# GpSimd issues the key pages of a paged attention cache, the sync engine the values

## The chip, the cores and the metric

The kernel runs on one core of one Trainium2 chip. The metric is the device time of one execution in microseconds. Five engines work at once, each on its own in-order stream of instructions: TensorE (PE; its weight loads are shown as PEld), VectorE (DVE), ScalarE (ACT), GpSimd (POOL) and SyncE (SP, which here only issues transfers). SP, ACT and POOL can issue DMAs. They are carried out by 16 DMA engines, which share the work of all queues.

## The reference, cut to what matters

One inference step of a two-layer decoder. Layer 0 is stick-breaking attention, layer 1 a diagonal state-space layer, and a gated MLP with a short convolution follows each. A prompt group (512 tokens) and a sample group (8 sequences of 8 new tokens, each with 2048 cached tokens) run through the same weights. The change touches the part in which the sample group reads its cache of 128 pages, 16 for each sequence. A page is 128 keys x 16 heads x 64 floats, 512 KB, and there is as much of values:

```
page_table = permutation(n_pool)[:8 * 16].reshape(8, 16)
k_all = cache_k[0][page_table]          # (8, 2048, 16, 64), values alike
z = (q . k) / 8 + bias                  # per head
log_keep = log_sigmoid(-z)              # causal
between = cumsum(log_keep, reverse) - log_keep
o = exp(log_sigmoid(z) + between) @ v
```

The scan over keys runs from the last key to the first, so the keys of a page must stand in their order along the columns of the scores.

## The kernel before, in words

In `attention_layer`, `sample_cache` (a generator) walks over the 128 pages in pairs. For page i, `load_k(i)` takes a buffer `kp` (128 partitions x 4 x 256 floats, one of KBUF = 4) and fills it by four DMAs, one for each quarter j. A quarter holds four of the 16 heads, 1 KB of each key, and goes to the 32 partitions 32j to 32j+31, four keys to a partition. By KSPLIT (line 45), SP issues the quarters 0, 1 and 2, and GpSimd quarter 3. Before that, each of the two reads the page's number from the table into a register (`page_id`). `load_v(i)` lets GpSimd issue one DMA of 512 KB into `vp` (one of VBUF = 4), 4 KB for each of 128 partitions.

`turn(i)` lets VectorE transpose `kp` in blocks of 32 x 32 into `kt` (two buffers, line 425), and then calls `load_k(i + 4)`, which has to wait for this transpose since it fills the same buffer. TensorE forms the scores z of a page in 16 matmuls (line 447). ScalarE takes two sigmoids of them (lines 455, 456), VectorE scans and multiplies (459, 460), TensorE transposes the weights back (469), ScalarE copies them (471), and TensorE multiplies them with the values into `po` (478). At line 457 GpSimd sets the one column `left[:, 256:]` to 1.0, from which the scan starts. At the end of a pair's round, `load_v` is called for the pair that reuses its `vp` buffers, and these wait for the products at line 478.

This stream runs beside the prompt's work: the generator `prompt_pair` and others are companions that the large matmuls step on by `tick`, so that on TensorE the small products of the sample lie between the large products of the prompt, in an order fixed at build time. TensorE works in that order: when the keys of a page are late, everything behind them on TensorE is late too. The projection weights come in units of 512 KB through SP (`load_unit`, line 169, three `raw` buffers), split into a high and a low half by ScalarE (140) and VectorE (141). A planner's simulated times set the order of each engine's instructions, so SP's stream mixes key quarters, weights and output rows. After the first pages, `raws["last"]` is the last DMA that SP issued for the keys, and later weight loads on SP are put behind it.

The stream starts at the end of the kernel's first 20 us. Its last pages are dealt with in the first MLP, `ffn(0, ...)`, which calls `between`, and from there `finish_sample`.

Of the kernel before, what the change touches and what calls it, by code (L numbers as in the profile page):

```python
# [17 lines left out]
P = 128  # L18
# [23 lines left out]
RAWX, KAFTER, XPRI, XN = 3, 1, 1, 2  # L42
QENG = 1
GUNITS = 0, 2, 4, 6
KSPLIT, VQ = (('SP', (0, 1, 2)), ('G', (3,))), 'G'
WEAVE, NPERIOD, IPERIOD = 2700, 6000, 1200
BIG = 4
ASTEPS, AEND = 44, 20
# [6 lines left out]
SB = {"gemm": 3, "tr": 2, "vy": 3}  # L55
SHARE = {"up": "vy"}
EARLY = 2
RL = 2
XA, XB = 0, 2
RAWU = 3, 4  # L60
QGROUPS = [[0, 1], [2, 3]]
# [31 lines left out]
def hybrid_kernel(  # L93
# [9 lines left out]
    V, S, G, T, SP = nc.vector, nc.scalar, nc.gpsimd, nc.tensor, nc.sync  # L103
# [46 lines left out]
    raws = {"pool": glob, "bufs": NRAW, "n": -1, "last": None, "chain": True, "views": {}}  # L150
# [50 lines left out]
    def norm_rows(xs, rows, gain, room=rows_tile, inplace=False):  # L201

        hs = [room()] * len(xs) if inplace else [room() for x in xs]
        ss = const.tile([P, len(xs)], F32, name="ss", tag="ss", bufs=3)
        for i, x in enumerate(xs):
            S.activation(hs[i][:rows], x, AF.Square, accum_out=ss[:rows, i:i + 1])
        r = rsqrt(const, ss, len(xs), rows, 1.0 / D, "nr", 3)
        if inplace:
            hs = xs
        for i, x in enumerate(xs):  # L210
            V.scalar_tensor_tensor(hs[i][:rows], x, r[:rows, i:i + 1], gain[:rows], ALU.mult, ALU.mult)
        return hs
# [86 lines left out]
    def attention_layer(sp, sps):  # L299
# [53 lines left out]
        def queries(b, eng=G):  # L353
            t = Qb[b % 2]
            for j in range(4):
                (eng.copy if eng == S else eng.tensor_copy)(t[32 * j:32 * j + 32, :, DS * j:DS * j + DS], Qc[32 * j:32 * j + 32, :, b * DS:(b + 1) * DS])
            return t
# [20 lines left out]
        def columns(ptag, perm):  # L378

            ps = sps.tile([P, 8, NS], F32, name="psc", tag=ptag, bufs=2)  # L380
            for c in range(8):
                T.transpose(ps[:, c, :], perm[:NS, c].rearrange("p j r -> p (j r)"), ident[:NS, :NS])
            return ps
# [3 lines left out]
        last_dma = {}  # L387

        def page_id(eng, idx):

            with tc.issue_after(last_dma[eng].ins) if eng in last_dma else nullcontext():
                return eng.value_load(idx, min_val=0, max_val=cache_k.shape[1] - 1)

        def sample_cache():

            pages = [(b, m, e) for b in range(DB) for m in range(NPG // 2 - 1, -1, -1) for e in (1, 0)]
            kps, kts, vps = {}, {}, {}
            Q = prev = po = before = None

            def number(i):  # L400
                b, m, e = pages[i]
                return pt[0:1, b * NPG + 2 * m + e:b * NPG + 2 * m + e + 1]

            def load_k(i):
                if i < len(pages):
                    kps[i] = sp.tile([P, 4, 256], F32, name="kp", tag="kp", bufs=KBUF)

                    for eng, js in KSPLIT:
                        eng = {'SP': SP, 'G': G, 'S': S}[eng]
                        r = page_id(eng, number(i))  # L410
                        page = cache_k[0, bass.ds(r, 1)].rearrange("o (kk kb) (j h) d -> j (o kk) kb (h d)", j=4, kb=4)
                        for j in js:
                            last_dma[eng] = eng.dma_start(kps[i][32 * j:32 * j + 32], page[j])  # L413

            def load_v(i):
                if i < len(pages):
                    vps[i] = sp.tile([P, D], F32, name="vp", tag="vp", bufs=VBUF)
                    eng = {'SP': SP, 'G': G, 'S': S}[VQ]
                    r = page_id(eng, number(i))
                    last_dma[eng] = eng.dma_start(vps[i], cache_v[0, bass.ds(r, 1)].rearrange("o k h d -> (o k) (h d)"))  # L420

            def turn(i):
                if i < len(pages):
                    kts[i] = sp.tile([P, 4, 8, 32], F32, name="kt", tag="kt")
                    V.transpose(kts[i].rearrange("p a c k -> p (a c k)"), kps.pop(i).rearrange("p a c -> p (a c)"))  # L425
                    load_k(i + KBUF)

            for i in range(KBUF):
                load_k(i)
            yield  # L430
            for i in range(2):
                load_v(i)
                turn(i)
            for i in range(0, len(pages) + 2, 2):
                if i < len(pages):
                    b, m, _ = pages[i]
                    start = m == NPG // 2 - 1
                    if start:
                        Q = queries(b, G if i or not QENG else S)

                    z = sps.tile([P, 512], F32, name="z", tag="sz", bufs=2)
                    for e in (1, 0):
                        x = i + 1 - e
                        kt = kts.pop(x)
                        for half in range(2):
                            for h in range(4):
                                T.matmul(z[32 * h:32 * h + 32, e * P:(e + 1) * P].rearrange("p (k a) -> p a k", a=4),  # L447
                                         Q[:, 2 * h + half, :], kt[:, :, 2 * h + half, :], start=half == 0, stop=half == 1)
                        turn(x + 2)
                        if e:  # L450
                            yield
                    sg = sp.tile([P, 256], F32, name="sg", tag="sg")

                    left = sp.tile([P, 257], F32, name="left", tag="left")
                    S.activation(left[:, :256], z[:, :256], AF.Sigmoid, bias=nbias_r, scale=-0.125)
                    S.activation(sg, z[:, :256], AF.Sigmoid, bias=bias_r, scale=0.125)
                    G.memset(left[:, 256:], 1.0)
                    back = left[:, ::-1]
                    V.tensor_tensor_scan(back, back, back, 1.0 if start else prev[:, 0:1], ALU.mult, ALU.min)
                    V.tensor_tensor(sg, sg, left[:, 1:], ALU.mult)  # L460
                    prev = left
                    now = i, b, m, z, sg
                    yield
                else:
                    now = None
                if before:
                    i0, b0, m0, z0, sg0 = before
                    for e in range(2):
                        T.transpose(z0[:, (2 + e) * P:(3 + e) * P], sg0[:, e * P:(e + 1) * P], ident)
                    wT = sp.tile([P, 2, P], F32, name="wT", tag="wT")  # L470
                    S.copy(wT.rearrange("p e f -> p (e f)"), z0[:, 256:])  # L471
                    yield
                    if m0 == NPG // 2 - 1:
                        po = sps.tile([P, 256], F32, name="po", tag="so")
                    for e in (1, 0):
                        v = vps.pop(i0 + 1 - e)
                        for h in range(4):
                            T.matmul(po[32 * h:32 * h + 32].rearrange("p (j d) -> p j d", j=4),  # L478
                                     wT[:, e, 32 * h:32 * h + 32],
                                     v.rearrange("p (j h d) -> p h j d", j=4, h=4)[:, h],  # L480
                                     start=m0 == NPG // 2 - 1 and e == 1, stop=m0 == 0 and e == 0)
                    if m0 == 0:
                        o = sp.tile([P, 256], F32, name="o", tag="wT")
                        S.copy(o, po)
                        S.dma_start(o_scr[:, b0], o)
                    yield
                for x in range(i + 2, i + 4):
                    load_v(x)
                before = now
# [206 lines left out]
        with pool_(name="start", bufs=2) as wp, pool_(name="start_ps", bufs=5, space=PSUM) as psp:  # L696
# [9 lines left out]
            with tc.high_priority():  # L706
# [8 lines left out]
                h, = norm_rows([xres[NT][:NS]], NS, gain)  # L715
# [31 lines left out]
            sample_query(1)  # L747
            raws["chain"] = False
            stream = sample_cache()
            with tc.issue_after(raws["last"].ins) if KAFTER else nullcontext():  # L750
                next(stream)
            raws["last"] = (None, raws["last"], last_dma[SP])[RL]
            ps = columns("sz", perm)
            with tc.high_priority():
                V.tensor_copy(Qc, ps)
# [949 lines left out]
    samp = sctx.enter_context(pool_(name="samp", bufs=2, side="right"))  # L1705
    samp_ps = sctx.enter_context(pool_(name="samp_ps", bufs=1, space=PSUM, side="right"))
    finish_sample, start = attention_layer(samp, samp_ps)

    def between():
# [36 lines left out]
```

## Time and profile before

| | |
|---|---|
| median of 3 runs | 1868.32 us (1867.57 to 1873.78) |
| the profiled execution's own time | 1855.74 us |
| its span, first to last instruction | 1854.0 us |
| mean granted TensorE clock | 0.962 of full speed |
| TensorE, VectorE, ScalarE, GpSimd busy | 92%, 62%, 39%, 20% of the span |
| moved by DMA | 297.42 MB, 160 GB/s over the span |

The page has one row for each engine with its busy time, and rows that cut the span into 40 equal slices, each digit a busy share in tenths; PEclk is the clock that TensorE was granted. The waits view tells for each engine at which line it sat idle and what ended that. The windows view gives busy time, the granted clock, the busy share of the 16 DMA engines and the bytes that they moved, for any stretch. The share can come out a little over 1.

### The profile page before, as it was taken

How to read it: one execution, taken by the hardware profiler on the slowest of the kernel's cores; microseconds unless marked ns; L12 is line 12 of the kernel's file. 1: busy time of each engine (PE TensorE's matmuls, PEld its weight loads, DVE VectorE, ACT ScalarE, POOL GpSimd, SP SyncE). 2: the span in 40 equal slices, each digit the busy share in tenths (PEclk: the TensorE clock that was granted, in tenths of full speed). 3: DMA queues.
4: the chain of work that ended last, by engine and by line, in shares of the span. 5: the costliest groups of instructions: out<-in, count | busy, mean ns of one | idle time of the engine just before them, and what ended most of it. 6: DMA issues, size and time to landing. Idle time of an engine off the chain costs nothing. (4 is left out here: it accounts for less than half of the span.)

```text
span 1854.0 us, 35632 instructions
## 1 busy us (share of the span) xinstructions
PE 1706.5 (92%) x12754; PEld 1419.9 (77%) x12754; DVE 1152.0 (62%) x2016; ACT 726.9 (39%) x1392; POOL 369.6 (20%) x676
## 2 busy tenths in 40 slices
PE   5988889989898998997999899899999999999999
PEld 3766566666545785896888889789878989989897
DVE  7445676676776666798668786765446544444443
ACT  5323434444443363432334534445433423323231
POOL 3132222222221110066123232001010100000000
PEclk8989999989988997998999999999999999999999
DMA  8799999999999682624375736455322322232221
GB/s 253 197 245 261 261 253 249 259 261 255 265 257 234 159 220 93 170 72 130 106 144 155 186 119 163 124 162 160 119 86 69 92 81 86 76 92 80 81 80 64
DMA packets 303301, 297.42 MB, mean 160 GB/s; under 512 B 58520, under 2 KB 250993, under 8 KB 303124
## 3 DMA queue, kind: packets, MB, share of 16 engines
q1 hardware_dynamic: 277074, 209.89, 43.1%
q0 software_dynamic: 24896, 84.20, 16.7%
q8 instruction: 101, 1.65, 0.4%
q10 hardware_dynamic: 1154, 1.05, 0.2%
q14 instruction: 76, 0.62, 0.1%
HBM read 268.93 MB, written 26.13 MB: 159 GB/s over the span
## 5 line engine op out<-in xcount | busy, mean ns | idle before, releaser
L862 PE MATMUL up<-hT,whi 128*128 128x256 f32 (+2 forms) x1344 | 407.3, 303 | 10.9 <-DVE gf L982 5.4
L141 DVE TENSOR_TENSOR wlo<-raw,whi 128x1024 fp32r<-128x1024 f32 x203 | 253.2, 1250 | 253.3 <-ACT whi L140 249.4
L863 PE MATMUL up<-hT,whi 128*128 128x256 f32 (+2 forms) x1344 | 403.4, 300 | 0.0
L864 PE MATMUL up<-hT,wlo 128*128 128x256 f32 (+2 forms) x1344 | 403.0, 300 | 0.0
L140 ACT CAST whi<-raw 128x1024 fp32r<-128x1024 f32 x206 | 215.3, 1048 | 351.4 <-PE up L863 151.0
L862 PEld LDWEIGHTS up<-hT,whi 128*128 128x128 f32 x1344 | 256.9, 191 | 20.1 <-DVE gf L982 6.9
L863 PEld LDWEIGHTS up<-hT,whi 128*128 128x128 f32 x1344 | 257.0, 191 | 3.1 <-issue 0.6
L864 PEld LDWEIGHTS up<-hT,wlo 128*128 128x128 f32 x1344 | 256.9, 191 | 1.5
L425 DVE STREAM_TRANSPOSE kt<-kp 128x1024 f32<-128x1024 f32 x128 | 157.9, 1238 | 145.4 <-DMA kp<-in_cache_k_dram 109.6
L447 PE MATMUL z<-kt,Qb 128*32 128x128 f32 x2048 | 100.4, 291 | 50.2 <-DVE kt L425 43.4
L268 PE MATMUL dn<-whi,g 128*128 128x512 f32 x352 | 137.3, 401 | 7.8 <-DVE xres L1059 5.0
L269 PE MATMUL dn<-wlo,g 128*128 128x512 f32 x352 | 140.8, 400 | 0.3 <-DVE wlo L141 0.3
L270 PE MATMUL dn<-whi,g 128*128 128x512 f32 x352 | 139.1, 398 | 0.0
L968 POOL COPY cst<-apad 128x2 f32<-128x2 f32 x44 | 36.7, 835 | 497.8 <-ACT apad L956 497.8
L447 PEld LDWEIGHTS z<-kt,Qb 128*32 128x32 f32 x2048 | 62.6, 114 | 78.5 <-DVE kt L425 40.0
L413 POOL DMA_DIRECT2D kp<-in_cache_k_dram x128 | 73.0, 571 | 238.7 <-DVE kt L425 99.7
L420 POOL DMA_DIRECT2D vp<-in_cache_v_dram x128 | 72.1, 563 | 187.6 <-PE po L478 118.2
L268 PE MATMUL psg<-whi,hT 128*128 128x256 f32 (+1 forms) x320 | 105.8, 332 | 0.3 <-DVE slo L606 0.3
L269 PE MATMUL psg<-wlo,hT 128*128 128x256 f32 (+1 forms) x320 | 103.9, 325 | 0.0
L270 PE MATMUL psg<-whi,hT 128*128 128x256 f32 (+1 forms) x320 | 102.4, 323 | 0.0
L478 PE MATMUL po<-vp,wT 128*32 128x256 f32 x1024 | 90.9, 414 | 0.8 <-ACT wT L471 0.4
L268 PEld LDWEIGHTS dn<-whi,g 128*128 128x128 f32 x352 | 66.2, 189 | 25.5 <-DVE xres L1059 5.9
(482 smaller groups left out, 3345.2 us busy)
## 6 DMA issues: line engine op xcount, KB each, us to landing
vp<-in_cache_v_dram POOLq DMA_DIRECT2D x128, 512.0 KB, 8.8
kp<-in_cache_k_dram SPq DMA_DIRECT2D x384, 128.0 KB
raw<-in_ffn_w_up_dram SPq DMA_DIRECT2D x96, 512.0 KB
raw<-in_ffn_w_down_dram SPq DMA_DIRECT2D x48, 512.0 KB
kp<-in_cache_k_dram POOLq DMA_DIRECT2D x128, 128.0 KB, 7.4
raw<-in_attn_w_qkv_dram SPq DMA_DIRECT2D x64, 128.0 KB
raw<-in_attn_w_o_dram SPq DMA_DIRECT2D x16, 512.0 KB
raw<-in_ssm_w_glu_dram SPq DMA_DIRECT2D x32, 256.0 KB
```

The lines of the kernel that those rows point to most:

```text
L140: S.copy(hi, src)
L141: eng.tensor_tensor(lo, src, hi.bitcast(F32), ALU.subtract)
L268: T.matmul(ps, x[0], whi, start=st, stop=False)
L269: T.matmul(ps, x[0], wlo, start=False, stop=False)
L270: T.matmul(ps, x[1], whi, start=False, stop=sp_)
L413: last_dma[eng] = eng.dma_start(kps[i][32 * j:32 * j + 32], page[j])
L425: V.transpose(kts[i].rearrange("p a c k -> p (a c k)"), kps.pop(i).rearrange("p a c -> p (a c)"))
L447: T.matmul(z[32 * h:32 * h + 32, e * P:(e + 1) * P].rearrange("p (k a) -> p a k", a=4), Q[:, 2 * h + half, :], kt[:, :, 2 * h + half, :], ...
L478: T.matmul(po[32 * h:32 * h + 32].rearrange("p (j d) -> p j d", j=4), wT[:, e, 32 * h:32 * h + 32], v.rearrange("p (j h d) -> p h j d", j= ...
L862: T.matmul(ps[:, :t1 - t0], w[0][:, k, :], hi, start=k == 0, stop=False)
L863: T.matmul(ps[:, :t1 - t0], w[0][:, k, :], lo, start=False, stop=False)
L864: last_mm["PE"] = T.matmul(ps[:, :t1 - t0], w[1][:, k, :], hi, start=False, stop=k == KC - 1)
```

## The change

GpSimd issues all four quarters of a key page, in the order 0, 2, 1, 3, and reads the page number once. The page in memory is described with other dimensions: key = 8n + a, with a, of size 8, outermost, and n, of size 16, inside it. As before, the elements fill the buffer in order, so that partition 4a + b of a quarter (b = 0 to 3) holds the keys 8n + a for n = 4b to 4b + 3. The matmul writes its columns so that the scores stand in the order of the keys again. SP issues the value pages. VectorE, not GpSimd, sets the column of `left`. `raws["last"]` becomes the last DMA of GpSimd.

```diff
-KSPLIT, VQ = (('SP', (0, 1, 2)), ('G', (3,))), 'G'
-RL = 2
...
-                    for eng, js in KSPLIT:
-                        eng = {'SP': SP, 'G': G, 'S': S}[eng]
-                        r = page_id(eng, number(i))
-                        page = cache_k[0, bass.ds(r, 1)].rearrange("o (kk kb) (j h) d -> j (o kk) kb (h d)", j=4, kb=4)
-                        for j in js:
-                            last_dma[eng] = eng.dma_start(kps[i][32 * j:32 * j + 32], page[j])
+
+                    r = page_id(G, number(i))
+                    page = cache_k[0, bass.ds(r, 1)].rearrange("o (n a) (j h) d -> j a (o n) (h d)", j=4, a=8)
+                    for j in (0, 2, 1, 3):
+                        last_dma[G] = G.dma_start(kps[i][32 * j:32 * j + 32], page[j])
...
-                    eng = {'SP': SP, 'G': G, 'S': S}[VQ]
-                    r = page_id(eng, number(i))
-                    last_dma[eng] = eng.dma_start(vps[i], cache_v[0, bass.ds(r, 1)].rearrange("o k h d -> (o k) (h d)"))
+                    r = page_id(SP, number(i))
+                    last_dma[SP] = SP.dma_start(vps[i], cache_v[0, bass.ds(r, 1)].rearrange("o k h d -> (o k) (h d)"))
...
-                                T.matmul(z[32 * h:32 * h + 32, e * P:(e + 1) * P].rearrange("p (k a) -> p a k", a=4),
-                                         Q[:, 2 * h + half, :], kt[:, :, 2 * h + half, :], start=half == 0, stop=half == 1)
+                                T.matmul(z[32 * h:32 * h + 32, e * P:(e + 1) * P].rearrange("p (b k a) -> p k a b", b=4, k=4),
+                                         Q[:, 2 * h + half, :], kt[:, :, 2 * h + half, :].rearrange("p k (a b) -> p k a b", b=4), start=half == 0, stop=half == 1)
...
-                    G.memset(left[:, 256:], 1.0)
+                    V.memset(left[:, 256:], 1.0)
...
-            raws["last"] = (None, raws["last"], last_dma[SP])[RL]
+            raws["last"] = last_dma[G]
```

## Rows read from the trace of the kernel before

**Rows 1.** The page: busy time by engine, and the DMA engines' share in 40 slices.

```profile
PE 1706.5 (92%) x12754; PEld 1419.9 (77%) x12754; DVE 1152.0 (62%) x2016; ACT 726.9 (39%) x1392; POOL 369.6 (20%) x676
...
DMA  8799999999999682624375736455322322232221
```

**Rows 2.** Windows: stretch, length, busy us (instructions) by engine, granted clock, DMA share, GB/s.

```profile
60.00:700.00 640.00, 570.51 (x5441) 401.79 (x5434) 415.49 (x657) 262.63 (x591) 156.03 (x344) 0.93 0.98 245
100.00:600.00 500.00, 438.27 (x4364) 297.43 (x4363) 327.35 (x500) 202.23 (x486) 131.56 (x288) 0.92 1.04 255
420.00:450.00 30.00, 30.00 (x287) 20.38 (x288) 23.32 (x38) 13.54 (x31) 9.57 (x21) 1.00 1.08 263
500.00:540.00 40.00, 33.58 (x294) 17.92 (x295) 27.18 (x38) 15.72 (x39) 11.56 (x27) 0.70 1.04 253
672.00:674.50 2.50, 2.50 (x23) 2.50 (x22) 2.50 (x3) 1.09 (x3) 0.36 (x2) 1.00 1.04 394
26.00:34.00 8.00, 5.55 (x16) 3.64 (x16) 6.23 (x9) 4.97 (x9) 4.58 (x5) 0.79 0.84 207
```

**Rows 3.** TensorE's waits from 60 to 700: total us, times, longest.

```profile
PE z L447 <- DVE kt L425: 43.4, 24, 5.1
```

**Rows 4.** What the transpose at line 425 waited for, 60 to 700: us, times.

```profile
  DMA kp<-in_cache_k_dram: 107.8, 48
```

**Rows 5.** DMA queues and issues, 60 to 700 (q0 GpSimd's, q1 SP's).

```profile
q1 hardware_dynamic: 89406, 72.35, 49.7%
q0 software_dynamic: 24000, 82.07, 47.2%
...
vp<-in_cache_v_dram POOLq DMA_DIRECT2D x126, 512.0 KB, 8.8
kp<-in_cache_k_dram SPq DMA_DIRECT2D x366, 128.0 KB
kp<-in_cache_k_dram POOLq DMA_DIRECT2D x122, 128.0 KB, 7.4
```

**Rows 6.** Queue q0 and what it issued, 672 to 674.5.

```profile
q0 software_dynamic: 206, 0.78, 81.5%
...
vp<-in_cache_v_dram POOLq DMA_DIRECT2D x1, 512.0 KB, 5.1
```

**Rows 7.** Lines 413 and 420 on GpSimd: durations in ns, min/median/max.

```profile
L413 POOL DMA_DIRECT2D kp<-in_cache_k_dram x118: 552/570/588, 62.1 to 639.3; - x118
...
L420 POOL DMA_DIRECT2D vp<-in_cache_v_dram x126: 537/563/574, 64.7 to 683.5; - x126
```

**Rows 8.** GpSimd's timeline: two issues back to back; a second value page.

```profile
24.86 1.10 POOL L413 DMA_DIRECT2D kp<-in_cache_k_dram  x2
...
104.57 0.56 POOL L420 DMA_DIRECT2D vp<-in_cache_v_dram  x1 [0.70 <-PE z L447]
```

**Rows 9.** GpSimd's waits, 60 to 700.

```profile
POOL vp L420 <- PE po L478: 118.2, 40, 32.7
...
POOL left L457 <- DVE left L459: 32.5, 18, 6.2
```

**Rows 10.** SP's timeline: a weight unit, and the MLP's first weights.

```profile
181.85 2.07 SPq L169 DMA_DIRECT2D raw<-in_attn_w_qkv_dram  x4
...
599.77 30.79 SPq L169 DMA_DIRECT2D raw<-in_ffn_w_up_dram  x5
```

**Rows 11.** GpSimd's timeline: the longest wait of a value page.

```profile
624.21 0.56 POOL L420 DMA_DIRECT2D vp<-in_cache_v_dram  x1 [32.66 <-PE po L478]
```

**Rows 12.** Lines by form, 60 to 700: busy us, mean ns, idle before.

```profile
L447 PE MATMUL z<-kt,Qb 128*32 128x128 f32 x2024 | 99.7, 291 | 50.2 <-DVE kt L425 43.4 <-DVE hn_ss L125 4.1 <-DVE rs_y L135 2.3
...
L469 PE MATMUL z<-ident,sg 128*128 128x128 f32 x128 | 29.5, 309 | 4.4 <-DVE sg L460 4.2
```

**Rows 13.** Line 457 on GpSimd, 60 to 700: durations in ns.

```profile
L457 POOL MEMSET left<- x62: 98/99/118, 70.3 to 678.9; 128x1 f32 x62
```

## The prediction, made blind

> **What bounds the kernel now.** I read the page first [rows 1]. TensorE is busy 92% of the span, but the row of slices shows something it doesn't have elsewhere: from slice 1 to slice 12 the DMA engines are full, and then never again. That is the stretch in which the sample reads its cache. So the windows come next [rows 2]: from 60 to 700 us TensorE is busy 570.5 of 640 us, idle 69.5, at a granted clock of 0.93; from 100 to 600 the DMA share is 1.04 at only 255 GB/s. Full engines need not mean full bandwidth, so I looked for stretches with other traffic. From 672 to 674.5, when the last key page has landed, the same share moves 394 GB/s, most of it a value page [rows 2, 6]. From 26 to 34, when the first key pages come in, 0.84 moves 207. Sixteen engines times share over rate gives the engine time of a megabyte: 16 x 1.04 / 255 = 65 us in the stage, 16 x 0.84 / 207 = 65 for the first key pages, 16 x 1.04 / 394 = 42 without keys. So it is the key quarters that make the transfers slow. The stage moves 72.35 + 82.07 MB and a little more [rows 5], 156.5 MB in all (245 GB/s x 640 us); at 65 us that is 156.5 x 65 / 16 = 636 us of all engines, which is the stage's length. The stage is as long as its transfers take.
>
> How this reaches TensorE is in the waits: the transpose of a page waited 107.8 us for keys, in 48 of 126 pages [rows 4], and TensorE 43.4 us for the transpose [rows 3]; with two waits in which another VectorE instruction came last, line 447 lost 50.2 of the 69.5 us [rows 12]. The clock is the second loss. Where no page is late TensorE is busy all the time at 1.00 (420 to 450), and in the worst part, 500 to 540, with 6.4 us idle, it is granted 0.70 [rows 2]. [...]
>
> **The change part by part.**
>
> *Keys.* Before, each of the 488 quarters in the stage is described with 32 groups of keys outermost on both sides, now with 8 on the side of the cache. If that makes 8 shares of it, consecutive quarters go to partitions 0 to 31, 64 to 95, 32 to 63, 96 to 127, and can run side by side, each on its own engines. No row shows a quarter dealt in this way. Its engine time per megabyte lies between 42 us (no keys, [rows 2]) and 65 (as now). What is needed is little: at the pace of a TensorE that never waits for keys, 640 - 50 = 590 us, the 156.5 MB may take 16 x 590 / 156.5 = 60 us a megabyte. I take a value under that, since GpSimd's own queue, whose traffic is four parts values and one part keys, already moves a megabyte in 0.472 x 16 x 640 / 82.07 = 59 us beside SP's 0.497 x 16 x 640 / 72.35 = 70 us [rows 5]. So keys no longer set the pace.
>
> [...]
>
> *What the lost wait is worth.* Of the 50 us at line 447 I count 37: three quarters, as VectorE, busy 415 of 640 us and in order, will be late for some pages itself. Of the 40 us of clock I count 18, somewhat under half, since low stretches follow idle ones and not all idling goes. Together 55; bounds 0 and 50 + 40 = 90.
>
> *GpSimd's queue.* It issues 4 x 128 quarters where it issued 128 quarters and 128 value pages: 256 more at 0.57 us [rows 7], 146 us, spread over 640 us in which it is busy 156. Two quarters one behind the other took 1.10 us, and a new page number costs 0.70 us [rows 8], so a page needs 4 x 0.57 + 0.70 = 3.0 us, against a page each 640 / 126 = 5.1 us, or 4.6 at the new pace. The last quarter goes out 1.7 us after the first. With four buffers a page is asked for three pages ahead, some 14 us, of which issue, landing (7.4 us now, [rows 5]) and transpose take 12. I take 0, and price the rest in the third rival. At the start twelve more quarters stand among GpSimd's weight splits: between 0 and 12 x 0.57 = 6.8 us, I take 0, as TensorE still has projections to do before its first keys.
>
> [...]
>
> *SP's queue.* It loses 384 issues and gets 128, and moving the values takes GpSimd's 118.2 us of waits for line 478 [rows 9] to SP. Behind a waiting value page now stand weight units, output rows, and the next value page; TensorE waits for the weights. A wait is 3 us on average (118.2 / 40), a unit is issued in about 2 us [rows 10], and the list of TensorE's waits in the stage names no weight tile; I take 0. The long wait, 32.7 us at 624 [rows 11], lies where the attention ends and five units of the MLP's weights go out between 600 and 631 [rows 10]. If they came behind it, up to 30 us would go back; the planner knows that wait and orders by it, so I take 0 and keep the 30 for the range. The value pages themselves need 5.1 to 8.8 us [rows 5, 6] and are asked for as soon as line 478 frees a buffer, two pairs ahead of their use.
>
> *The small edits.* 64 settings of a column move to VectorE: 0.10 us each on GpSimd [rows 13], 6 us of VectorE time if it is no faster, none where it waits anyway; with it go GpSimd's 32.5 us of waits at line 457 [rows 9], which would hold up keys. I take 0. The scores' columns are now written 32 elements apart, not 4: line 447, at a step of 4, takes 291 ns, line 469, at a step of 1, 309 [rows 12], so the step shows no price; 0. `raws["last"]` on GpSimd's queue orders nothing on SP; weights may go out ahead of the first pages: 0.
>
> **The sum.** The profiled execution took 1855.7 us, with 1.7 us around its span of 1854.0. Less 55 that is 1801. The median of the runs shown stands 12.6 us above that execution, so I say 1813.
>
> **The rivals.**
>
> *TensorE keeps much of its idling.* Keys come in time, but VectorE and ScalarE then end last at each step of the stream, and the clock stays low: gain 6 to 20 us, 1848 to 1862. For it: VectorE's 65%. Against it: the 30 us from 420 to 450 at 100% of TensorE and full clock with the same work [rows 2].
>
> *Nothing moves.* The engines are the bound by their number, or the reads of 1 KB from each key are what is slow and not their way in: 65 us a megabyte remain, 1868. For it: queue q1's rows are mostly such reads. Also here if the transfer isn't cut as I think.
>
> *GpSimd becomes the bound, or one half of the engines does.* The slower case is a quarter that costs GpSimd more than (5.1 - 0.7) / 4 = 1.1 us instead of 0.57; from there on pages come late however fast they land. At 1.3 us a page takes 5.9 and the stage 126 x 0.8 = 100 us more: 1970. Against it: 588 ns at most. The same side is reached if all quarters fall to the same eight engines: these would carry the keys, 64 MB, and half of the remaining 92.5, 110 MB, in 110 x 42 / 8 = 578 us at best, still no loss, but slower from 46 us a megabyte on; at 55 it is 756, and the time 1868 + 116 = 1984. No view shows which engines serve a DMA. I give GpSimd 0.07 and the half 0.05.
>
> **How the numbers follow.** The forecast, a gain of 20 to 100 us, gets 0.70, idling kept 0.08, nothing moves 0.10, the slower cases 0.12. What a measurement can tell from no change is 0.3%, 5.6 us. Faster takes 0.70, 0.08 and a little of the third: 0.80. Same 0.09, slower 0.11. The forecast's own range is 1778 (both bounds, 90 us) to 1848; below, 1768 would take the clock wholly back with what other idling there is. Upward I go to 1866, which takes in the kept idling and the 30 us of late weights; the slower cases, and most of "nothing moves", stay out.
>
> **What would show it.** Right: from 100 to 600 us on the old axis, a DMA share well under 1 at 270 GB/s or more; the transposes' wait for keys under 30 us; TensorE's wait at line 447 under 15; the granted clock from 60 to 640 at 0.96 or more; the end of the stage some 55 us earlier, and all behind it moved, not changed. Wrong: a share of 1 at 250 GB/s (nothing moves); GpSimd's issues longer than 1 us, or GpSimd with no idle time (it is the bound); SP waiting for line 478 with TensorE waiting for weights behind it.

## The result, and the profile after

The changed kernel takes 1798.74 us (median, 1791.93 to 1801.45), the kernel before beside it 1867.94: a ratio of 0.9643, 95% interval 0.9609 to 0.9676, so 69 us faster. 1813 was forecast. The profiled execution took 1791.93 us, its span 1790.2 against 1854.0. Lines have moved: 413 is now 410, 416 issues the values (420 before), 421 is the transpose (425), 443 the key product (447), 474 the value product (478), 453 the column of `left` (457), 455 the scan (459).

The page, busy time by engine and the DMA slices, answers to [rows 1]:

```profile
PE 1669.1 (93%) x12754; PEld 1401.0 (78%) x12754; DVE 1154.4 (64%) x2080; ACT 727.8 (41%) x1394; POOL 549.2 (31%) x868
...
DMA  8599888877899946233757454554222222232221
```

TensorE has the same 12754 matmuls and is busy 37.4 us less: they ran at full clock more often (mean granted clock 0.972, before 0.962). The other 26.4 of the 63.8 us of span were idle time (147.5 before, 121.1 now). The DMA engines now have spare time from the fifth slice to the eleventh.

Windows of the changed kernel, columns as in [rows 2]:

```profile
60.00:640.00 580.00, 537.87 (x5494) 386.47 (x5492) 420.07 (x710) 267.73 (x598) 327.86 (x528) 0.97 0.87 270
60.00:700.00 640.00, 580.37 (x5840) 415.56 (x5839) 461.19 (x829) 288.17 (x638) 327.86 (x528) 0.95 0.82 255
100.00:600.00 500.00, 474.59 (x4822) 341.48 (x4820) 380.63 (x656) 246.69 (x551) 284.05 (x459) 0.99 0.88 274
580.00:700.00 120.00, 78.16 (x805) 49.26 (x804) 73.99 (x170) 33.08 (x70) 34.18 (x53) 0.73 0.67 209
```

From 100 to 600 a megabyte now takes 16 x 0.88 / 274 = 51 us of engine time, not 65 [rows 2]. TensorE is busy 475 of 500 us there (438 before) at 0.99 of its clock (0.92). The last row is a loss that the kernel before doesn't have: TensorE is idle 42 us of 120, at 0.73 of its clock. This is called the tail below; the same stretch before, at the same columns:

```profile
580.00:700.00 120.00, 114.55 (x877) 91.49 (x874) 79.85 (x151) 55.01 (x94) 16.52 (x42) 0.99 0.76 200
```

VectorE's and TensorE's waits, 60 to 700 (us, times, longest), two queries of one view, answer to [rows 3, 4]:

```profile
DVE kt L421 <- DMA kp<-in_cache_k_dram: 6.5, 5, 3.6
...
PE po L474 <- ACT wT L467: 12.7, 15, 5.3
PE z L443 <- DVE kt L421: 9.1, 4, 3.5
```

The transposes wait 6.5 us for keys (107.8), TensorE 9.1 for the transpose (43.4); its wait for the attention weights that ScalarE copies, 12.7, is now longer than that. GpSimd's issues and the queues, answering to [rows 5, 7]:

```profile
L410 POOL DMA_DIRECT2D kp<-in_cache_k_dram x488: 647/647/663, 72.4 to 630.2; - x163
```

```profile
q1 hardware_dynamic: 63975, 96.83, 48.7%
q0 software_dynamic: 39040, 64.24, 32.5%
...
vp<-in_cache_v_dram SPq DMA_DIRECT2D x125, 512.0 KB, 6.0
kp<-in_cache_k_dram POOLq DMA_DIRECT2D x488, 128.0 KB, 5.2
```

Keys land in 5.2 us (7.4), values in 6.0 (8.8), while more bytes move in the same time (274 GB/s from 100 to 600, before 255).

Where TensorE's order went: the costliest group of the output projection, before from 600 to 640, and after from 440 to 480:

```profile
L270 PE MATMUL psg<-whi,o_lo 128*128 128x512 f32 x42 | 16.6, 395 | 0.0
```

```profile
L267 PE MATMUL psg<-wlo,o_hi 128*128 128x512 f32 x42 | 17.1, 408 | 0.0
```

The prompt's attention is done some 150 us earlier, while the last key product only moved from 682.9 to 638.0. In TensorE's instruction list 57.5 of 64 pairs of pages stood ahead of the output projection; now 39.5 do. This order is planned at build time, and it moves with the queue that issues what (43.5 in e6 below, 54 in e7); the planner had drawn the prompt's work ahead.

### The profile page after: what moved, and what is told of

Its sections match the earlier page's. It is cut to its first block, busy times and chain, and to the rows that moved or that the text cites. A ratio compares the mean times of both kernels' runs of the same rounds, so it can differ in the third digit from the quotient of the medians.

```text
span 1790.2 us, 34994 instructions
## 1 busy us (share of the span) xinstructions
PE 1669.1 (93%) x12754; PEld 1401.0 (78%) x12754; DVE 1154.4 (64%) x2080; ACT 727.8 (41%) x1394; POOL 549.2 (31%) x868
## 5 line engine op out<-in xcount | busy, mean ns | idle before, releaser
L410 POOL DMA_DIRECT2D kp<-in_cache_k_dram x512 | 331.6, 648 | 229.2 <-DVE kt L421 131.0
L266 PE MATMUL psg<-whi,hT 128*128 128x256 f32 (+1 forms) x320 | 100.6, 316 | 0.5 <-DVE hT L139 0.5
L267 PE MATMUL psg<-wlo,hT 128*128 128x256 f32 (+1 forms) x320 | 99.4, 311 | 0.0
L268 PE MATMUL psg<-whi,hT 128*128 128x256 f32 (+1 forms) x320 | 98.4, 309 | 0.0
L443 PE MATMUL z<-kt,Qb 128*32 128x128 f32 x2048 | 85.7, 291 | 9.1 <-DVE kt L421 9.1
L474 PE MATMUL po<-vp,wT 128*32 128x256 f32 x1024 | 77.6, 416 | 14.0 <-ACT wT L467 12.7
L443 PEld LDWEIGHTS z<-kt,Qb 128*32 128x32 f32 x2048 | 57.0, 116 | 32.9 <-issue 10.6
L267 PEld LDWEIGHTS dn<-wlo,g 128*128 128x128 f32 x352 | 66.7, 190 | 15.9 <-DVE wlo L139 0.7
```

Source lines behind the costliest of these rows:

```text
L266: T.matmul(ps, x[0], whi, start=st, stop=False)
L267: T.matmul(ps, x[0], wlo, start=False, stop=False)
L268: T.matmul(ps, x[1], whi, start=False, stop=sp_)
L410: last_dma[G] = G.dma_start(kps[i][32 * j:32 * j + 32], page[j])
```

## The experiments

All twelve have an interval from runs beside the kernel before, whose medians lie between 1865.3 and 1868.9 us in all sets. "A megabyte" is engine time, 16 x share / rate from 100 to 600. The traces of e3, e7 and e9 are of executions 15, 17 and 11 us above the medians in the table. The edits are given in short form, and "shares", as in the name of e1, are the parts into which I took one DMA to be divided among the engines: an assumption, since no view shows them or which engines serve a DMA.

| run | ratio, 95% interval | median us | a megabyte, us |
|---|---|---|---|
| changed kernel | 0.9643, 0.9609 to 0.9676 | 1798.74 | 51 |
| e1, 16 shares | 0.9833, 0.9796 to 0.9870 | 1836.88 | 61 |
| e2, neighbours | 0.9810, 0.9771 to 0.9850 | 1833.84 | 61 |
| e3, order 0, 1, 2, 3 | 0.9824, 0.9789 to 0.9860 | 1833.77 | 61 |
| e4, 8 groups, old queues | 1.0158, 1.0120 to 1.0196 | 1897.42 | 54 |
| e5, 16 groups, dealt | 0.9829, 0.9789 to 0.9869 | 1837.02 | 62 |
| e6, values moved only | 1.0138, 1.0097 to 1.0179 | 1888.30 | 62 |
| e7, SP quarter 3 | 1.0165, 1.0143 to 1.0188 | 1894.74 | 65 |
| e8, SP quarter 1 | 0.9940, 0.9918 to 0.9962 | 1855.74 | 60 |
| e9, order held | 0.9749, 0.9715 to 0.9784 | 1825.04 | 51 |
| e10, held, faster stream | 0.9877, 0.9847 to 0.9907 | 1847.30 | 50 |
| e11, held, 16 shares | 0.9885, 0.9845 to 0.9925 | 1847.01 | 62 |
| e12, memset on GpSimd | 0.9806, 0.9770 to 0.9841 | 1831.76 | 51 |

**e1, e2, e3, e5: what made the keys fast.** TensorE's order is that of the changed kernel in all four. e5 has 16 groups outermost, not 8 (key = 16n + a).

```diff
 e1 -j a (o n) (h d)", j=4, a=8      +"o (kk kb) (j h) d -> j (o kk) kb (h d)", j=4, kb=4
 e2 -"o (n a) (j h) d                +"o (a n) (j h) d
 e3 -for j in (0, 2, 1, 3):          +for j in (0, 1, 2, 3):
 e5 -j=4, a=8)                       +j=4, a=16)
```

> The changed kernel, but the key quarters are described with 32 groups of keys outermost again (4 neighbouring keys to a partition), and the matmul as before. All issues, their queues, their order 0, 2, 1, 3 and TensorE's order of instructions stay those of the changed kernel. Theory A (what made the transfers fast is that a quarter is dealt to 8 engines, each with its own way into its partitions, and two quarters run side by side): the gain from the rate goes, the engine time of a megabyte from 100 to 600 us rises from 51 us to 58 or more, the transposes wait for keys 60 us or more (6.5 in the changed kernel), time 1825 to 1880. Theory B (what made them fast is GpSimd's queue, which gathers the 1 KB reads into larger packets where SP's sends them one by one): the shares don't matter, 1799 +- 6.

> The changed kernel with 8 outermost, but each of the eight groups takes 16 neighbouring keys (key = 16a + n, not 8n + a); the matmul writes as before the change. Theory A: the way into the partitions is the same, 1799 +- 8. Rival C (the dealing of neighbouring keys to different engines is part of the gain, because the reads of a page then spread better): slower by 1% or more, 1817 and up, with a higher engine time per megabyte.

> The changed kernel with the quarters in the order 0, 1, 2, 3, nothing else. Theory A, with the engines taken eight at a time in turn: quarters 0 and 1 then go by two sets of engines into the same half of the ways in, so the rate falls to that of before, 58 us a megabyte or more, time 1825 to 1880. If only the number of shares matters: 1799 +- 6.

> [...] Queues, order of quarters and TensorE's order stay those of the changed kernel. Theory A (two quarters side by side on 8 engines each is what counts): as with 16 shares of neighbours, 1837 +- 8, engine time 60 us a megabyte. Rival C (dealing neighbours is what counts, for the reads): 1799 +- 8, 51 us a megabyte.

Measured: all four near 1835 us and 61 us a megabyte. Theory A's numbers hold in e1, e3 and e5; theory B (the queue) and rival C (the dealing) fall. What stands of theory A is its numbers; its engines and their ways into the partitions are in no view. One expectation missed: in e1 the transposes wait 9.6 us for keys, not 60 or more. The slow transfers show in the values instead, in TensorE's waits:

```profile
PE po L474 <- DMA vp<-in_cache_v_dram: 22.7, 9, 5.2
```

In e2 theory A seemed to fall, for rival C's number came, but the run isn't what I took it for. GpSimd's issues, of e2 and then of e3:

```profile
L410 POOL DMA_DIRECT2D kp<-in_cache_k_dram x456: 550/550/567, 76.6 to 638.2; - x152
```

```profile
L410 POOL DMA_DIRECT2D kp<-in_cache_k_dram x451: 647/647/663, 79.0 to 638.3; - x151
```

With eight outermost, dealt, an issue takes 647 ns (e3, the changed kernel); with 16 or 32 outermost 550 (e1, e5). GpSimd's queue from 60 to 700, for the same 488 quarters, again of e2 and then of e3:

```profile
q0 software_dynamic: 23424, 63.99, 40.1%
```

```profile
q0 software_dynamic: 39040, 64.24, 41.9%
```

That is 48 packets a quarter in e2, as in e1 and e5, and 80 in e3, as in the changed kernel. So e2's 8 x 16 neighbours, which lie one behind the other in memory, gave the issue time and the packets of e1. I take it that they were read as one dimension of 128, which is an inference. It is e1 once more, in time too (1833.84 us, e1 1836.88). Neighbouring keys at 80 packets a quarter were not tried.

e3 is the cleanest: the same instructions, two of them swapped in each page. Its windows row from 100 to 600, and the wait for keys:

```profile
100.00:600.00 500.00, 473.87 (x4671) 341.38 (x4673) 367.87 (x636) 241.98 (x542) 268.35 (x432) 0.96 0.98 255
```

```profile
DVE kt L421 <- DMA kp<-in_cache_k_dram: 40.5, 17, 4.4
```

The engines are full again at the old 255 GB/s. Quarters 0 and 1 one behind the other cost 35 us against 0 and 2. The packets in the traces, counted from 100 to 600 us, say how: a 4 KB packet of a key quarter takes 198 ns on average in the changed kernel, 254 in e3 and 256 in e1, with no fewer of them under way at once in e3 (ten or more in 25% of the time, in the changed kernel in 18%). So the packets themselves were slower where a quarter was followed by the other one of its half of the partitions (e3), and where it was described with 32 groups outermost (e1).

**e4, e7, e8: quarters of eight groups on SP's queue.**

```diff
 e4 (on the kernel before) -(o kk) kb (h d)", j=4, kb=4 +a (o n) (h d)", j=4, a=8; the matmul as in the change
 e7 -for j in (0, 2, 1, 3): G  +G: (0, 2, 1), SP: (3,)
 e8 -for j in (0, 2, 1, 3): G  +G: (0, 2, 3), SP: (1,)
```

> The kernel before with the new description of a quarter alone (8 outermost, keys dealt, the matmul's new order of columns): SP still issues quarters 0, 1 and 2, GpSimd quarter 3 and the values; TensorE's order of instructions is that of before. If SP's queue also takes the engines eight at a time in turn: faster, 1810 to 1850. If SP's queue always takes the same eight engines: these carry three quarters of the keys (48 MB of 64) and half of the rest, 102 of 156.5 MB, so slower than before, 1880 to 2050. Theory B: 1868 +- 6.

> The changed kernel with quarter 3 given back to SP: GpSimd issues 0, 2, 1, SP quarter 3 and the values, all with 8 outermost. With three and two issues a page, the planner puts 54 of 64 pairs ahead of the output projection (39.5 in the changed kernel), and none are left at the end without other work beside them. Theory E (what the changed kernel still loses is its tail: from 580 to 700 us TensorE is idle 42 of 120 us and at 0.73 of its clock, because the last pages run alone): 1740 to 1785. Rival (SP's quarter always takes the same eight engines and meets quarter 2 on the way in, so the rate falls back): 1800 to 1850.

> As the run before, with SP issuing quarter 1 and GpSimd 0, 2, 3. [...] Theory E again: 1740 to 1785; the rival 1800 to 1850.

Measured: e4 is 1.6% slower than before, and its 1897.42 us lie in the 1880 to 2050 of the second case; which engines SP's queue takes is in no view. Theory B misses here too. Its windows row shows engines at rest while keys are late:

```profile
100.00:600.00 500.00, 417.11 (x4134) 282.86 (x4122) 305.61 (x469) 187.42 (x460) 136.46 (x276) 0.88 0.82 241
```

```profile
DVE kt L425 <- DMA kp<-in_cache_k_dram: 147.1, 57, 6.1
```

In the packets of the traces it shows too: ten or more packets of SP's quarters are under way together in 26% of the time from 100 to 600 before, and in 3% in e4, though SP has three quarters to issue for each page; for GpSimd's quarters in the changed kernel it is 18%. I read this as quarters of eight groups that hardly ran side by side on SP's queue in e4, and did on GpSimd's in the changed kernel.

e7 and e8 miss theory E, and its rival as well: e7 by 45 us, e8 by 6. They differ in which quarter SP issues, and by 39 us: e8 with quarter 1 takes 1855.74 us, e7 with quarter 3 1894.74. Why is not shown. Both have a fault in TensorE's waits (e7, then e8):

```profile
PE po L475 <- DMA vp<-in_cache_v_dram: 84.0, 46, 6.0
```

```profile
PE po L475 <- DMA vp<-in_cache_v_dram: 46.5, 34, 3.7
```

Values go out late: in the traces a value page is issued some 5 us (median) after its buffer has come free, in the changed kernel 0.4. Ahead of it in SP's queue there now stands a key quarter. How much of the 39 us these late values make isn't parted off.

**e6: the values moved, nothing else.**

```diff
-KSPLIT, VQ = (('SP', (0, 1, 2)), ('G', (3,))), 'G'
+KSPLIT, VQ = (('SP', (0, 1, 2)), ('G', (3,))), 'SP'
```

> The kernel before with only the value pages moved to SP; the keys stay as they were (SP three quarters, GpSimd one, 32 groups outermost). TensorE's order moves with it: before, 57.5 of the 64 pairs of pages stand ahead of the output projection, now 43.5 (39.5 in the changed kernel), so pages are read while the output projection runs. Theory D (of the 69 us, 31 come from this order, which lets the slow transfers run on through 580 to 640 us, and not from any faster transfer): 1837 +- 12, the engine time of a megabyte staying at 60 to 65 us, DMA share from 580 to 640 up from 0.67 to over 0.95. Rival (the 31 us come from GpSimd's queue carrying the keys): 1868 +- 8.

Measured: 1888 us, both wrong. Queues and TensorE's waits, 60 to 700:

```profile
q1 hardware_dynamic: 104004, 130.50, 79.3%
q0 software_dynamic: 5712, 15.61, 10.2%
```

```profile
PE po L478 <- DMA vp<-in_cache_v_dram: 46.0, 26, 4.0
```

Keys and values in one queue make the values late here: TensorE waits 46.0 us for them (0.3 before, 1.2 in the changed kernel), a value page is issued 12.2 us (median) after its buffer has come free (1.6 before), and the engines rest 11% of the time (share 0.89 from 100 to 600). GpSimd, too, stands 308.9 us at line 457 here, but it isn't its quarter that is late: all 63 of the transposes' waits for keys end with one of SP's. Moved alone, then, the values cost 23 us. The change moves the keys off SP's queue with them: all keys here, all values there.

**e9, e10, e11: TensorE's order.**

```diff
 e9  +last_z[0] = T.matmul(z[...   (the stream's page product)
     +with tc.issue_after(last_z[0].ins):
     +    rows[c] = project_pair(pool, psp, c, xT)
 e10 the same around the output projection, WEAVE 2700 -> 2400
 e11 e9 with e1's description and matmul
```

> The changed kernel, with TensorE's order held: each projection of the prompt is put behind the last page product that the stream has put out so far, so that the planner can't draw the prompt's work ahead. 51 of 64 pairs of pages stand ahead of the output projection (39.5 in the changed kernel), the last ones beside the MLP. Theory E, in a form in which SP's queue stays as the change made it (the changed kernel loses up to 60 us in its tail, where the last pages run alone): 1745 to 1785, TensorE idle under 20 us from 580 to 700. Rival F (the pages then ask for more than the transfers give, and what the tail loses now is lost in waits for keys and values ahead of it): 1790 to 1830.

> As the run before, with the output projection held too and the stream stepped on every 2400 cycles, not 2700: 57 of 64 pairs ahead of the output projection, all 64 before the MLP. The 156.5 MB must then come in some 500 us, 310 GB/s. If the transfers can do that (310 GB/s from 580 to 640 us in the changed kernel's tail): 1740 to 1775. If not, value pages and keys are late and it is slower than the run before by 10 us or more.

> The order held as in the first run of this set, with 16 shares and neighbours as in the kernel before, so with slow transfers. Theory D' (of the gain of the change, the 31 us that stayed with 16 shares are owed to the order, which draws prompt work ahead while the pages are slow): with the order held these 31 us go, 1850 to 1885. Rival (they are owed to keys and values having a queue each): 1837 +- 8.

Measured: e9 is at 1825, rival F's number. The tail is gone, as theory E had it, but its loss came up earlier: e9's windows from 580 to 700, from 100 to 600, and the latter in two parts, then the changed kernel's second part:

```profile
580.00:700.00 120.00, 106.97 (x1079) 83.43 (x1077) 87.78 (x199) 54.88 (x90) 38.97 (x67) 0.95 0.75 233
```

```profile
100.00:600.00 500.00, 454.03 (x4530) 312.56 (x4522) 348.06 (x605) 214.37 (x509) 285.41 (x454) 0.92 0.83 260
100.00:150.00 50.00, 28.79 (x374) 15.46 (x366) 24.63 (x38) 8.73 (x22) 33.76 (x55) 0.64 0.99 322
150.00:600.00 450.00, 425.25 (x4156) 297.10 (x4156) 323.43 (x567) 205.64 (x487) 251.65 (x399) 0.95 0.81 253
```

```profile
150.00:600.00 450.00, 425.84 (x4265) 300.80 (x4257) 344.67 (x586) 226.41 (x497) 253.49 (x410) 0.99 0.86 268
```

From 580 to 700 it is idle 13 us instead of 42; from 100 to 600 idle 46 instead of 25, and the clock is 0.92 instead of 0.99. Of these 46 us, 21 lie between 100 and 150, at 0.64 of the clock and with the engines full (0.99). There the pages run alone: until 140, TensorE has nothing but the products of the stream, with the projections held behind them. From 150 to 600 both kernels are idle 24 to 25 us, e9 at a clock of 0.95, not 0.99. So the edit has moved the stretch in which the pages run alone from the end to the start, and it doesn't test theory E fairly: its number is missed, but what the changed kernel would take with other work beside all its pages isn't shown.

e10 is 22 us slower than e9, as its second case has it, but not for that reason: TensorE waits 4.7 us for values and the transposes 15.2 for keys, at a share of 0.83. It is the key products that wait more still (36.1 us for the transposes). Packed denser, the stream's chain over four engines may be late by itself; that is argued, not shown.

e11 against e9 is the price of slow transfers in one order, 22 us. Against e1 it is 10 us slower with intervals that overlap, 3 us faster than D' allowed and 2 slower than its rival. So how the 31 us that stayed in e1 divide is open: between the order, the parted queues and the column of `left`, which e1 also leaves to VectorE (e12).

**e12: the small edit.**

```diff
-                    V.memset(left[:, 256:], 1.0)
+                    G.memset(left[:, 256:], 1.0)
```

> The changed kernel with the column of 1.0 set by GpSimd again, as before the change. If the small edit is worth nothing: 1799 +- 6. If GpSimd's wait at that line, 32.5 us in the kernel before, holds up key quarters behind it: 1805 to 1830, with the transposes' wait for keys up from 6.5 us.

Measured: 33 us slower at the same 51 us a megabyte, 2 us beyond the second case. Waits from 60 to 700, GpSimd's, VectorE's and TensorE's:

```profile
POOL left L453 <- DVE left L455: 17.7, 7, 6.1
```

```profile
DVE kt L421 <- DMA kp<-in_cache_k_dram: 40.7, 16, 4.1
```

```profile
PE z L465 <- DVE sg L456: 31.9, 8, 7.3
```

GpSimd waits for the scan of an earlier pair before it may set the column, and the quarters behind it go out late: the first of a page 2.5 us (median) after its buffer has come free, in the changed kernel 0.5. VectorE then stands in a transpose that waits for keys (6.5 us in the changed kernel), and the scans behind that transpose are late for TensorE. The planner's order also differs a little (38 pairs ahead of the output projection, not 39.5), and what that costs isn't parted off.

## Why the prediction was right, and where not

- *The transfers bound the stage, and the keys made them slow:* right. 51 us a megabyte is inside the bounds 42 to 65 and under the 60 that was needed. That it takes both the eight dealt groups and quarters of different halves of the partitions one behind the other is shown by e1, e3 and e5: each undoes one of the two, and loses 35 to 38 of the 69 us (61, 61 and 62 us a megabyte against 51). That two quarters then run "each on its own engines" was my reading; no view shows it.
- *The lost wait:* 37 us of idling and 18 of clock were counted; 26 and 37 came. No run shows the 40 us of clock that the 18 were taken from; what the runs showed in its place is a granted clock of 0.99 from 100 to 600, 0.92 before, and 37.4 us less of TensorE's busy time. The sum is near, 55 for 64 in the profiled executions, its split is not. That is in part luck: the sum knows nothing of the tail, where TensorE is idle 42 us (5 before), nor that 33 us hang on the column of `left`. I had counted under half of the clock because a low stretch had come with idle time (0.70 from 500 to 540, 6.4 us idle, [rows 2]); from 100 to 600, where keys are in time, nearly all of it came back.
- *GpSimd's queue:* right that it doesn't bind (it waits 131.0 us at line 410 for the transposes that free its buffers); an issue costs 0.65 us, not 0.57, 3.3 us a page.
- *SP's queue:* right that TensorE doesn't wait for weights, though SP stands longer than I thought at line 474, as the row of its waits from 60 to 700 says:

```profile
SPq L416 <- PE po L474: 233.0, 56, 15.7
```

- *The small edits at 0:* wrong for the column of `left`. That its waits, the 32.5 us of [rows 9], would hold up keys was seen, but priced at nothing; without this edit the change gains 37 us, not 69 (e12), with the planner's part in that unknown.
- *"All behind it moved, not changed":* wrong. I took TensorE's order as fixed, when it is planned from the queues. The new order made the tail of 580 to 700 us, and the last key product came 45 us earlier, not 55. The one order that was held against it, e9's, was 26 us worse.
- *The slower rivals:* of the second, half of the engines as the bound, no view can tell; e4, with the quarters of eight groups on SP's queue, is 1.6% slower, with ten or more packets of these quarters under way in 3% of the time. On GpSimd's queue it is 18%, and there the change gains.

## What to carry to other kernels

A full DMA share at a low rate was the sign here (1.04 at 255 GB/s): compare the engine time of a megabyte with a stretch of other traffic (65 us against 42), and if it is longer, look at how a transfer is described (e1: 51 to 61 us), and what follows it in its queue (e3: 51 to 61). Put on one queue only transfers that wait for the same thing, and no small work that waits for another: in e6 value pages behind keys went out 12.2 us after their buffers had come free (1.6 before), and e12's column went with 33 us. When a queue changes and a planner orders the engines, compare the instruction lists before any argument that takes the order as given.

## What the runs showed of the hardware that I had not expected

Two nested groups that lie one behind the other in memory seem to have acted as one dimension in e2: its issues (550 ns), its 48 packets a quarter and its time (1833.84 us) are those of e1, within 3 us. Quarters of eight dealt groups gain on GpSimd's queue (1798.74 us, e1 1836.88), and on SP's they lose (e4, 1.6%), with ten or more of their packets under way in 3% of the time (26% for the quarters of before). Quarter 3 on SP's queue came out 39 us slower than quarter 1 (e7, e8), part of which may be the late values. And one column set per pair of pages, moved to another engine's queue, went with 33 us, part of which may be the planner's.
